# A hybrid attention and convolution block: the decay gates' matmuls are moved from between two quads to inside the next one

## The chip, the core and the metric

The kernel runs on one NeuronCore of a Trainium2 chip. The metric is the device time of one execution in microseconds; the time before is the median of three runs. The engines are TensorE (PE in the profile), VectorE (DVE), ScalarE (ACT), GpSimd (POOL) and SyncE (SP, which only issues DMAs here).

## What is computed

One layer on a sequence of 1024 tokens of width 1024, all in float32: an RMS norm, one wide input projection, then side by side a gated linear attention in both directions (4 heads, keys of 128, values of 256) and a gated convolution of width 3; both results are concatenated, projected back, added to the input and normed once more. Cut to the parts that the change touches:

```python
proj = einsum('bsd,de->bse', rmsnorm(x, norm_g), w_in)
q, k, v, z_a, lr_f, lr_b, b_gate, c_gate, h_c, z_c = split(proj, ...)
# the decay gates, for each direction
g_f = log_sigmoid(einsum('bsr,re->bse', lr_f, w_gk_f) + b_gk_f) / 16
# inside the attention: sums of g over each chunk of 64 tokens
b = cumsum(g, axis=3)
# the convolution group
u = c_gate * h_c
conv = conv_w[0] * u[t-1] + conv_w[1] * u[t] + conv_w[2] * u[t+1] + conv_b
y_c = b_gate * conv * silu(z_c)
```

## The kernel before

The work runs in three stages. Up to about 125 us the input is normed and turned into column tiles and the values of the heads are computed. From there to 606 us the rest of the projection is computed in twelve *quads*. After that come the attention and the output projection. The change lies in the second stage.

A quad (`quad`, line 544) computes four blocks of 128 output columns for all 1024 tokens. Each product is a Strassen-like scheme of seven products of quarter size (Winograd's form), and each float32 factor is split into a high and a low part, so that one product of two parts is three chains of matmuls. Of the seven first-level products of a block pair, one is done at a second level again, for both pairs of the quad together, with half as wide matmuls: that is `second` (line 505). So a quad is: `second` (its matmuls are 256 columns wide), then the first `pair` (line 402), then the second `pair`. The part `finish` of `second` runs inside the first pair, behind its first product.

`second` uses four banks of PSUM, `bx`, `by`, `bz` and `bw`, and writes `bx` and `by` twice. In order: line 525 (`bx`), 527 (`by`), 529 (`bz`), 531 (`bw`), 533 (`bx` again, added to what is there, after ACT's copy in line 526 has read it), 535 (`by` anew, after DVE's sum in line 528 has read it). Then the first pair's product of line 433 follows. A pair ends each of its last products with a DVE sum (`plus`, line 430); in the order of these sums the products are named p2, p7, p5 (used twice), p4 and p3. Ahead of its products a pair takes sums and differences of its raw weights on DVE (`comb`, line 407), and turns each operand into parts: a cast on ACT (line 152) and a difference on POOL (line 153).

The first eight quads are the convolution's: in the first pair the columns of c_gate and h_c, whose product `u` POOL makes (line 611); in the second pair the columns of z_c and b_gate, whose results go through `conv_y` (lines 614 to 641): the convolution (lines 619 to 621), a tanh on ACT (line 633) with two DVE operations behind it (lines 634 and 635), and a product on POOL (line 637). The other four quads compute q, k and z_a; behind their last sums stands a tanh with one DVE operation (lines 560 and 561).

The gates are cut into eight pieces, one for each head and direction, and one piece goes with each convolution quad. `gates` (line 568) does four matmuls of 64 rows and 512 columns into two banks of their own (line 577), for each half an ACT Abs (line 578) and a DVE operation (line 579) on the same bank, and one ACT Exp (line 580). `summed` (line 582) issues the ACT Ln (line 587, with a load of its table) and leaves five steps in the list `beside`: for each half a difference (line 597) and a scan of 512 (line 591 or 593), and then the DMA of `b` to DRAM (line 599). The next quad's first pair takes one step from the list behind each of its `plus` sums (`step`, line 396).

Nothing in this stage has an order written out by hand, but for `issue_after`, which queues an instruction behind another on the same engine. The framework's planner orders each engine's queue: it goes by the order of the program and by its own estimate of when operands and buffers are ready, and so may draw a later DVE operation forward into a hole. Tiles of one name take their buffers in the order of the program (`tmp` has nine). Each engine then runs its queue in order.

Of the kernel before, what the change touches and what calls it, by code (L numbers as in the profile page):

```python
# [37 lines left out]
def tile_hybrid_gla_shortconv(ctx, tc, x, norm_g, w_in, w_gk_f, b_gk_f, w_gk_b, b_gk_b,  # L38
# [40 lines left out]
    def weights(src):  # L79
        r = ws.tile([P, ND, P], F32, name="raw", bufs=4)  # L80
        r = r.rearrange("p c e -> p (c e)").rearrange("p (c e) -> p c e", e=src.shape[2])
        nc.sync.dma_start(r, src)
        return r
# [229 lines left out]
    def sums():  # L313
        for c in range(4):
            f01, f00, f11 = (joined(hb[d][s_], c) for d, s_ in ((0, 1), (0, 0), (1, 1)))
            minus(f01, f00, t1, c, f00)
            minus(f11, f01, t3, c, f01)
            minus(f11, f00, t2, c, f11)
            yield
# [21 lines left out]
    beside = sums()  # L341
# [32 lines left out]
    def s_tile():  # L374
        return ws.tile([P, 4, P], F32, name="s", bufs=3)
# [14 lines left out]
    def load(col):  # L390
        return weights(w_in[:, :, col:col + P])


    beside = []
# [110 lines left out]
    def second(x, y, h):  # L505

        b00, t1, t2, t3, b10, b11, t4 = h
        a00, a01, a10, a11 = x[:, 0:2], x[:, 2:4], y[:, 0:2], y[:, 2:4]
        f, g = s_tile(), s_tile()
        s2, s1, s3, s4 = f[:, 0:2], f[:, 2:4], g[:, 0:2], g[:, 2:4]  # L510
        o0 = part(x)
        V.tensor_tensor(s1, a10, a11, ALU.add)
        V.tensor_tensor(s2, s1, a00, ALU.subtract)
        o1 = part(f)
        V.tensor_tensor(s3, a00, a10, ALU.subtract)
        V.tensor_tensor(s4, a01, s2, ALU.subtract)
        o2 = part(g)
        o3 = part(a11)
        first_, last_ = (lambda o: tuple(a[:, 0:2] for a in o)), (lambda o: tuple(a[:, 2:4] for a in o))
        r = [wk.tile([P, 512], F32, name="r2", bufs=2) for _ in range(2)]  # L520
        lo, hi = slice(0, 256), slice(256, 512)
        w = tmp()
        p1, u = w[:, lo], w[:, hi]
        bx, by, bz, bw = (bank6()[:, lo] for _ in range(4))
        product(bx, first_(o0), b00, True, True)
        A.copy(p1, bx)
        product(by, first_(o1), t2, True, True)
        V.tensor_tensor(p1, by, p1, ALU.add)  # L528
        product(bz, first_(o2), t3, True, True)
        V.tensor_tensor(u, bz, p1, ALU.add)  # L530
        product(bw, last_(o1), t1, True, True)
        V.tensor_tensor(r[1][:, hi], bw, u, ALU.add)
        product(bx, last_(o0), b10, False, True)
        A.copy(r[0][:, lo], bx)
        product(by, o3, t4, True, True)
        V.tensor_tensor(r[1][:, lo], by, u, ALU.add)

        def finish():
            product(bw, last_(o2), b11, False, True)
            V.tensor_tensor(r[0][:, hi], bw, p1, ALU.add)  # L540

        return *r, finish

    def quad(cols_a, take_a, cols_b, take_b):
        xa, xb = load(cols_a[0]), load(cols_b[0])
        ra, rb, finish = second(xa[:, 4:8], xb[:, 4:8], h2)
        pair(xa, load(cols_a[1]), take_a, ra, finish, step)
        pair(xb, load(cols_b[1]), take_b, rb)

# [18 lines left out]
    def gates(h, d):  # L568

        bias = bgk[:, d, h:h + 1]  # L570
        dr = slice(d * 64, d * 64 + 64)
        b, m = u_tile()[:, 0:S], u_tile()[:, 0:S]
        for half in range(2):
            sl = slice(half * 512, half * 512 + 512)
            ps = bank()
            for i, w in enumerate((gk_hi, gk_lo)):
                T.matmul(ps, w[dr, h * DK:(h + 1) * DK], lr[half][dr], start=i == 0, stop=i == 1)
            A.activation(b[:, sl], ps, AF.Abs, bias=bias)
            V.tensor_scalar(m[:, sl], ps, bias, 0.0, ALU.add, ALU.min)
        return b, m, A.activation(b, b, AF.Exp, scale=-1.0)  # L580

    def summed(h, d, b, m, exp):

        with tc.issue_after(exp.ins):
            A.activation(b, b, AF.Ln, bias=1.0)

        def scan(b_, m_):
            if d == 0:  # L590
                V.tensor_tensor_scan(b_, smask, m_, 0.0, ALU.mult, ALU.add)
            else:
                V.tensor_tensor_scan(b_[:, ::-1], smask, m_[:, ::-1], 0.0, ALU.mult, ALU.add)

        for half in range(2):
            b_, m_ = (a[:, half * 512:half * 512 + 512] for a in (b, m))
            beside.append(lambda b_=b_, m_=m_: V.tensor_tensor(m_, m_, b_, ALU.subtract))
            beside.append(lambda b_=b_, m_=m_: scan(b_, m_))
        beside.append(lambda: nc.sync.dma_start(b_dram[h][d], b))
# [68 lines left out]
    for j in range(CW // P):  # L668
        u, *first_ = conv_u(j)
        args = *first_, *conv_y(j, u)  # L670
        quad(*args)
        summed(j // 2, j % 2, *gates(j // 2, j % 2))
    for h in range(NH):
        quad((Q0 + h * DK, K0 + h * DK), to_dram((q_dram[h], k_dram[h])),
             (Z0 + h * DV, Z0 + h * DV + P), silu2_to_dram(z_dram[h]))
# [373 lines left out]
```

## Time and profile before

| | |
|---|---|
| time, median of 3 runs | 901.11 us (897.99 to 902.21) |
| the profiled execution | 903.29 us, of which the span of the profile 901.2 us |
| PE busy | 865.7 us (96% of the span), 4452 matmuls |
| PE weight loads | 725.2 us (80%) |
| DVE busy | 713.4 us (79%) |
| ACT busy | 393.7 us (44%) |
| POOL busy | 448.2 us (50%) |
| mean granted TensorE clock | 0.986 of full speed |

A row of a timeline gives the start in us from the start of the span, the length in us, the engine, the line of the kernel, the operation, the tile that it writes and those that it reads, and shapes; in brackets stands how long the engine was idle before it, and which instruction it waited for. The lengths of matmuls overlap, since they are pipelined: the distance of two starts is what one costs.

### The profile page before, as it was taken

To read this page: it belongs to the slowest core of one execution; us is meant where nothing else is said; L and a number is where in the kernel's file an instruction comes from. 1 tells how busy PE (TensorE), PEld (TensorE's weight loads), DVE (VectorE), ACT (ScalarE), POOL (GpSimd) and SP (SyncE) were. 2 spreads that over 40 slices of the span, in tenths; PEclk is the share of its full clock that TensorE was granted. 3 is DMA by queue.
4 is the path that set the end of the run, shared out by engine and by line. 5 is a ranking of instruction groups with operands and counts; after the bars stand their busy time and mean duration, and the time that the engine had idled before them with its cause. 6 is when DMAs were issued, how large, how long until landed. Compare 5 with 4: busy or idle time off the path is not lost.

```text
span 901.2 us, 12971 instructions
## 1 busy us (share of the span) xinstructions
PE 865.7 (96%) x4452; PEld 725.2 (80%) x4452; DVE 713.4 (79%) x1283; ACT 393.7 (44%) x822; POOL 448.2 (50%) x391
## 2 busy tenths in 40 slices
PE   7999969999999999999999999999999999999996
PEld 6999958887887878787878888887878787888885
DVE  6879986888888888888888565666799989975754
ACT  5533233434445362635344342443365446542553
POOL 3368676757768576768665655520112212222231
PEclk9999969999999999999999999999999999999999
DMA  7521332222231313132233433468856344310122
GB/s 252 138 74 56 86 109 56 71 70 71 71 94 48 117 47 105 60 94 71 70 94 129 134 102 116 128 208 327 293 159 222 105 136 134 120 52 24 42 77 93
DMA packets 102163, 100.35 MB, mean 111 GB/s; under 512 B 10705, under 2 KB 82385, under 8 KB 101586
## 3 DMA queue, kind: packets, MB, share of 16 engines
q1 hardware_dynamic: 102098, 99.53, 35.0%
q8 instruction: 35, 0.57, 0.3%
q14 instruction: 30, 0.25, 0.1%
HBM read 71.20 MB, written 28.31 MB: 110 GB/s over the span
## 4 chain that ended last, share of the span: by engine, by line
PE 72%; DVE 17%; issue 4%; DMA 3%; POOL 2%; ACT 1%; SPq 0%; POOLq 0%; DVEq 0%; ACTq 0%
PE out L715 16%; PE pc L381 15%; PE pb L381 15%; PE pa L381 15%; PE po L872 3%; PE pu L917 2%; DVE tmp L304 1%; DVE tmp L635 1%; DVE tmp L430 1%; DVE f L304 1%; DMA k<-k_dram 1%; DVE s L407 1%; DMA raw<-in_w_in 1%; DVE xt L177 1%; DVE dd L820 1%
## 5 line engine op out<-in xcount | busy, mean ns | idle before, releaser
L153 POOL TENSOR_TENSOR a_lo<-s,a_hi 128x512 fp32r<-128x512 f32 x74 | 116.0, 1573 | 28.8 <-ACT a_hi L152 28.5
L153 POOL TENSOR_TENSOR a_lo<-tmp,a_hi 128x512 fp32r<-128x512 f32 x48 | 70.3, 1466 | 103.8 <-ACT a_hi L152 99.0
L153 POOL TENSOR_TENSOR a_lo<-raw,a_hi 128x512 fp32r<-128x512 f32 x84 | 111.2, 1327 | 14.8 <-ACT a_hi L152 14.8
L147 POOL TENSOR_TENSOR rs<-rs,mhalf 128x1 f32<-128x1 f32 x48 | 28.7, 598 | 142.6 <-DVE rs L146 135.2
L715 PE MATMUL out<-a_hi,y_hi 128*128 128x512 f32 x192 | 89.2, 465 | 0.5 <-ACT y_hi L152 0.5
L152 ACT CAST a_hi<-raw 128x512 fp32r<-128x512 f32 x108 | 63.8, 595 | 58.3 <-PE pc L381 17.2
L152 ACT CAST a_hi<-tmp 128x512 fp32r<-128x512 f32 x48 | 29.8, 621 | 122.8 <-DVE tmp L407 99.4
L715 PE MATMUL out<-a_hi,y_lo 128*128 128x512 f32 x192 | 77.1, 401 | 0.0
L715 PE MATMUL out<-a_lo,y_hi 128*128 128x512 f32 x192 | 77.0, 401 | 0.0
L827 POOL TENSOR_TENSOR kt<-kt,k 128x256 f32<-128x256 f32 x32 | 26.3, 821 | 97.7 <-ACT kt L824 70.8
L152 ACT CAST a_hi<-s 128x512 fp32r<-128x512 f32 x74 | 45.0, 617 | 47.4 <-PE pa L381 17.5
L381 PE MATMUL pa<-h_hi,a_hi 128*128 128x512 f32 (+1 forms) x128 | 47.7, 373 | 5.2 <-DVE tmp L528 2.8
L381 PE MATMUL pb<-h_hi,a_hi 128*128 128x512 f32 (+1 forms) x128 | 48.2, 376 | 4.5 <-DVE tmp L528 3.8
L381 PE MATMUL pc<-h_hi,a_hi 128*128 128x512 f32 (+1 forms) x128 | 48.0, 375 | 2.6 <-DVE tmp L528 2.6
L381 PE MATMUL pa<-h_hi,a_lo 128*128 128x512 f32 (+1 forms) x128 | 47.0, 367 | 0.7 <-POOL a_lo L153 0.7
L381 PE MATMUL pc<-h_lo,a_hi 128*128 128x512 f32 (+1 forms) x128 | 47.2, 369 | 0.0
L381 PE MATMUL pb<-h_hi,a_lo 128*128 128x512 f32 (+1 forms) x128 | 47.2, 369 | 0.0
L381 PE MATMUL pc<-h_hi,a_lo 128*128 128x512 f32 (+1 forms) x128 | 47.1, 368 | 0.0
L381 PE MATMUL pb<-h_lo,a_hi 128*128 128x512 f32 (+1 forms) x128 | 47.1, 368 | 0.0
L381 PE MATMUL pa<-h_lo,a_hi 128*128 128x512 f32 (+1 forms) x128 | 46.8, 365 | 0.0
L715 PEld LDWEIGHTS out<-a_hi,y_lo 128*128 128x128 f32 x192 | 36.4, 190 | 8.0
L717 DVE TENSOR_TENSOR res<-out,res 128x512 f32<-128x512 f32 x48 | 32.9, 686 | 12.4 <-PE out L715 12.3
(344 smaller groups left out, 2735.2 us busy)
## 6 DMA issues: line engine op xcount, KB each, us to landing
raw<-in_w_in SPq DMA_DIRECT2D x56, 512.0 KB, 4.0
raw<-in_w_out SPq DMA_DIRECT2D x16, 512.0 KB, 3.9
xt<-in_x SPq DMA_DIRECT2D x8, 512.0 KB, 8.4
yc_dram<-tmp SPq DMA_DIRECT2D x16, 256.0 KB, 2.0
b_dram<-u SPq DMA_DIRECT2D x8, 512.0 KB, 2.6
z_dram<-tmp SPq DMA_DIRECT2D x16, 256.0 KB, 2.4
s<-yc_dram SPq DMA_DIRECT2D x16, 256.0 KB, 3.9
raw<-in_x SPq DMA_DIRECT2D x8, 512.0 KB, 6.7
```

Source lines behind the costliest of these rows:

```text
L147: G.tensor_tensor(rs, rs, mhalf, ALU.pow)
L152: (e_hi.copy if e_hi is A else e_hi.tensor_copy)(hi, src)
L153: e_lo.tensor_tensor(lo, src, hi.bitcast(F32), ALU.subtract)
L177: V.scalar_tensor_tensor(xts[t][:, sl], xts[t][:, sl], rs, gb[:, sl], ALU.mult, ALU.mult)
L304: V.tensor_tensor(f, blk[0].bitcast(F32)[:, c], blk[1].bitcast(F32)[:, c], ALU.add)
L381: T.matmul(ps, a[x0][:, k], b_[x1][:, k], start=start and k == 0 and j == 0, stop=stop and k == n - 1 and j == 2, skip_group_check=not start)
L407: V.tensor_tensor(f, x0, x1, op)
L715: T.matmul(ps, a[:, j, :], w, start=j == 0 and i == 0, stop=j == 3 and i == 2)
L717: V.tensor_tensor(res[t][:, cs], ps, (xr if row0 == NT else res[t])[:, cs], ALU.add)
L827: G.tensor_tensor(kk, kk, k4, ALU.mult)
L872: T.matmul(o, l, m, start=j == 0, stop=j == len(mm) - 1)
L917: T.matmul(pu[:, d], ks[:, d], r["v"][:, t], start=True, stop=True)
```

## The change

In the convolution's quads the call of `gates` and `summed` moves from behind the quad into it, between `second` and the first pair. In the list `beside` an empty step goes ahead of the other steps, so that the first sum of the pair (behind p2) takes nothing, and the two differences, the two scans and the DMA stand behind the following sums, of the same quad as the gates.

```diff
-    def quad(cols_a, take_a, cols_b, take_b):
+    def quad(cols_a, take_a, cols_b, take_b, aside=lambda: None):
         xa, xb = load(cols_a[0]), load(cols_b[0])
         ra, rb, finish = second(xa[:, 4:8], xb[:, 4:8], h2)
+        aside()
         pair(xa, load(cols_a[1]), take_a, ra, finish, step)
         pair(xb, load(cols_b[1]), take_b, rb)
...
+        beside.append(lambda: None)
         for half in range(2):
             b_, m_ = (a[:, half * 512:half * 512 + 512] for a in (b, m))
             beside.append(lambda b_=b_, m_=m_: V.tensor_tensor(m_, m_, b_, ALU.subtract))
             beside.append(lambda b_=b_, m_=m_: scan(b_, m_))
         beside.append(lambda: nc.sync.dma_start(b_dram[h][d], b))
...
         u, *first_ = conv_u(j)
         args = *first_, *conv_y(j, u)
-        quad(*args)
-        summed(j // 2, j % 2, *gates(j // 2, j % 2))
+        quad(*args, lambda: summed(j // 2, j % 2, *gates(j // 2, j % 2)))
```

The amount of work on each engine stays the same. The first gates' matmuls now stand in the first quad instead of behind it, and the last in the eighth quad instead of ahead of the first Q/K quad.

## Rows read from the trace of the kernel before

**Rows 1.** PE's waits from 124 to 606 us: engine, bank and line, releaser: total, times, longest us

```profile
PE pb L381 <- DVE tmp L528: 3.8, 3, 1.9
...
PE pb L381 <- ACT tmp L526: 0.6, 1, 0.6
```

**Rows 2.** Timeline of PE near 207 us: start, length, operation, tiles, count [idle before]

```profile
204.99 0.49 PE L577 MATMUL out<-y_hi 64*128 64x512 f32 x1
...
206.11 0.39 PE L381 MATMUL pc<-h_hi,a_hi 128*128 128x256 f32 x1
...
209.65 0.28 PE L381 MATMUL pc<-h_hi,a_lo 128*128 128x256 f32 x1
210.84 0.38 PE L381 MATMUL pa<-h_hi,a_hi 128*128 128x256 f32 x1 [0.91 <-DVE tmp L528]
...
217.86 0.39 PE L381 MATMUL pc<-t_hi,a_hi 128*128 128x512 f32 x1
```

**Rows 3.** Timeline of DVE at the same place

```profile
206.68 0.68 DVE L430 TENSOR_TENSOR tmp<-pb,tmp 128x512 f32<-128x512 f32 x1
207.28 0.73 DVE L579 TENSOR_SCALAR u<-out,bgk 128x512 f32<-128x512 f32 x1
208.05 0.69 DVE L634 SCALAR_TENSOR_TENSOR th<-th,tmp 128x512 f32<-128x512 f32 x1
...
209.32 1.13 DVE L635 SCALAR_TENSOR_TENSOR tmp<-th,tmp 128x512 f32<-128x512 f32 x1
210.37 0.41 DVE L528 TENSOR_TENSOR tmp<-pa,tmp 128x256 f32<-128x256 f32 x1
```

**Rows 4.** Timeline of ACT at the same place

```profile
207.39 0.63 ACT L633 ACTIVATE th<-tmp 128x512 f32<-128x512 f32 x1 [0.95 <-DVE tmp L430]
...
208.49 0.37 ACT L526 COPY tmp<-pc 128x256 f32<-128x256 f32 x1
...
211.13 1.06 ACT L587 ACTIVATE u<-u 128x1024 f32<-128x1024 f32 x1
```

**Rows 5.** Timeline of POOL at the same place

```profile
206.88 1.31 POOL L153 TENSOR_TENSOR a_lo<-raw,a_hi 128x512 fp32r<-128x512 f32 x1
208.14 1.76 POOL L637 TENSOR_TENSOR tmp<-tmp 128x512 f32<-128x512 f32 x1
```

**Rows 6.** Timelines of DVE and POOL near 203 us

```profile
202.62 1.19 DVE L407 TENSOR_TENSOR s<-s,raw 128x512 f32<-128x512 f32 x1
203.73 1.23 DVE L407 TENSOR_TENSOR s<-raw 128x512 f32<-128x512 f32 x1
203.22 1.19 POOL L153 TENSOR_TENSOR a_lo<-raw,a_hi 128x256 fp32r<-128x256 f32 x1
```

**Rows 7.** Timeline of DVE between two Q/K quads

```profile
568.11 0.69 DVE L430 TENSOR_TENSOR tmp<-pb,tmp 128x512 f32<-128x512 f32 x1 [0.38 <-PE pb L381]
568.72 1.75 DVE L407 TENSOR_TENSOR tmp<-raw 128x512 f32<-128x512 f32 x1
570.40 0.68 DVE L561 SCALAR_TENSOR_TENSOR tmp<-tmp 128x512 f32<-128x512 f32 x1
571.00 0.41 DVE L528 TENSOR_TENSOR tmp<-pa,tmp 128x256 f32<-128x256 f32 x1
```

**Rows 8.** Timeline of DVE: the last product's sum at two other boundaries

```profile
165.00 0.67 DVE L430 TENSOR_TENSOR tmp<-pa,tmp 128x512 f32<-128x512 f32 x1
...
453.19 0.68 DVE L430 TENSOR_TENSOR tmp<-pb,tmp 128x512 f32<-128x512 f32 x1
```

**Rows 9.** Chain of work: start us, us, what; 18 matmuls of lines 535 and 433 together

```profile
170.39 3.73 PE pc L381 x18
...
292.93 5.29 PE pc L381 x18
...
457.35 3.74 PE pa L381 x18
```

**Rows 10.** PE by stretches of 2 us: stretch, PE busy (x), granted clock, DMA share, GB/s

```profile
294.00:296.00 2.00, 2.00 (x8) 0.50 0.08 30
```

## The prediction

> **What bounds the kernel now.** I read the page first (span, busy shares), then the list of who waited for whom on PE between 124 and 606 us, the chain of work, and last the timelines of PE, DVE, ACT and POOL around one place. PE is the bound: from 130 us to 606 us it runs almost without a gap. The list of its waits names one kind that counts, a product waiting for DVE's line 528, nine times, up to 1.9 us [rows 1] (one of three such lines, by the bank, with three waits each, and the only line of another kind). The first of the nine (at 128 us) is the start of the stage, before any quad's gates; the other eight stand at the eight places where a quad follows a convolution quad. I call these boundaries 1 to 8; boundary 2, near 207 us, is the model. Between two Q/K quads, where no gates stand, the list has no such wait.
>
> Boundary 2 on PE [rows 2]: the four gate matmuls run from 204.99 to 206.11 (1.12 us), then `second`'s first 30 narrow matmuls (lines 525 to 533) from 206.11. The last of them starts at 209.65, so they take 0.122 us each and PE could start line 535 at 209.77, which is 3.66 us after 206.11. It starts at 210.84. Line 535 writes the bank `by` anew, and so has to wait until line 528 has read it. PE thus loses 1.07 us here, with the gates' 1.12 us already spent ahead of it.
>
> Why line 528 is late [rows 3, 4, 5]: DVE runs the last product's sum (L430) at 206.68, then a gate operation (L579) at 207.28, L634 at 208.05 when ACT's tanh has come (207.39 + 0.63), the other L579, L635 at 209.32, and line 528 at 210.37. L635 takes 1.13 us because POOL holds the SBUF: POOL's second L637 ends at 208.14 + 1.76 = 209.90, and L635 ends 0.55 us after that. That POOL and DVE take turns is seen elsewhere [rows 6]: of two DVE operations back to back (202.62 and 203.73, 1.2 us each) the second waits for POOL's operation, which started between them and itself waited for the first. The Trainium skill (SBUF — State Buffer, section "SBUF: two separate sides") states that this pair of ports is an exclusive lock for a whole instruction. By that rule the trace agrees. The rows alone say that taking away the two L579 frees less than their length, since L635 ends with POOL and not with DVE's queue.
>
> From L430's start to line 535's start it is 210.84 - 206.68 = 4.16 us in boundary 2 and 457.35 - 453.19 = 4.16 us in boundary 8 [rows 2, 3, 8, 9]; the five between agree within 0.01. Boundary 1, where DVE isn't behind, has 170.39 - 165.00 = 5.39 us.
>
> **The change part by part.** *The gate matmuls on PE* (4 x 8) keep their number. They leave the eight boundaries ahead of `second` and go behind line 535. Ahead, their 1.12 us passed while DVE worked towards line 528: they were cover. Behind line 535 nothing is late (the rest of the quad has no wait), so each quad pays 1.12 us there: 8 x 1.12 = +8.96 us. Against it stands x, by which line 535 starts earlier after the end of the last quad. The change of the time is 8.96 minus the sum of the eight x.
>
> *What DVE does without the two L579.* PE comes to line 535 at 204.99 + 3.66 = 208.65. Line 528 is issued in the order that the planner gives DVE. The trace of before doesn't show this boundary without gates, but three Q/K boundaries are without them: there DVE has L430, L407 (a difference of raw weights for the next pair, 1.75 us beside POOL), L561 behind the tanh, L528, L407 [rows 7]. So while the tanh runs, L407 fills the hole in which L579 stood. Why not before: L407's `tmp` comes behind the one that ACT's line 526 fills (208.49, rows 4), and with 1.12 us of gate matmuls ahead that came too late. I take the same order with L634 for L561: L430, L407, L634, L528, L635. In boundary 2: L407 from 207.28, held until POOL's L153 ends (206.88 + 1.31 = 208.19), done 0.55 later at 208.74. POOL's L637, ready since 208.14, now takes its turn: 1.25 us, to about 209.95. L634 waits for that and ends 0.55 later at 210.5, line 528 runs 210.42 to 210.83, and line 535 starts at 210.88. So x = 210.84 - 210.88, about zero. The two L579 are gone and L407 and the lock have their place. This holds too if L407 isn't drawn in and L635 stays ahead of line 528: L637 follows L634, L635 follows L637, as before. Line 528 comes early only with no more than one locked operation in front of it. POOL's order around it hangs on the same L430, so boundaries 2 to 8 have x = -0.04 each. In boundary 1, POOL is further ahead relative to PE; the same steps give L407 to 167.0, L637 to 168.25, L634 to 168.8, line 535 at 169.2: x = 1.2. Sum of x: 1.2 - 7 x 0.04 = 0.9; **+8.0 us**.
>
> The bounds of x from both sides: at best line 535 doesn't wait at all, x = 210.84 - 208.65 = 2.19 in boundary 2 (19.7 over the eight, from the same rows of each); at worst three locked operations stand ahead (L407, L634, L635), each further one costing POOL's 1.25 and its own 0.55, x = -1.8.
>
> *PE's clock.* In boundary 4 two waits stood close, 0.6 us for ACT's L526 [rows 1] and the usual one for L528, and after them the granted clock was 0.50, the 1.2 GHz level, between 294 and 296 us [rows 10]; the 18 matmuls then took 5.29 us for 3.73 [rows 9], 1.56 us more. At boundaries 1 and 8, with one wait of under 1 us, the 18 took 3.73 and 3.74. In my order L533 waits for L526 (behind the tanh: 207.39 + 0.63 + 0.37, less overlap, 208.3 for 207.83: 0.45 us) and then line 535 for 1.9 us: more idle than boundary 4 had. The Trainium skill (TensorE: Matmul & The Clock Gate, section "What's actually happening") says that TensorE's idle state is the slow one and activity releases it. I take three more falls in seven boundaries, the middle between none and all: 3 x 1.56 = **+4.7 us**; range 0 to 10.9.
>
> *ACT's gate work* (two Abs, Exp, table, Ln) moves into the first pair. Before, it ends 7.2 us after the first gate matmul (212.19 - 204.99, rows 2, 4), with other work between. After, it would end at most 0.82 (line 535) + 7.2 = 8.0 us after line 535's start. The first sum (L597) stands on DVE behind p7's sum. p7's product starts 217.86 - 210.84 + 1.12 = 8.14 us after line 535 and ends 2.75 later, so the Ln is done and no DVE queue is held. If the casts for p7 stood wholly behind the Ln, PE would wait there up to 1.8 us (a pass of ACT like the tanh's 0.63, POOL's lower half 1.31: 9.94 for 8.14); I take zero, because its L407 now comes earlier and the cast is ready before the Abs. Range 0 to 1.8 a quad.
>
> *L579, sums and DMA.* Two L579 (2 x 0.73 us) and the later sums meet idle DVE in the first pair; p3's sum comes later by up to a scan, and POOL's product into `u` stands behind lower halves of the second pair's casts anyway, so the convolution isn't later. `b_dram`'s DMA moves back on SP as far as the last scan does, with the raw loads behind it, which are for the next quad: zero. Lost cover: if the convolution did get later, every us would come on L430 of the next boundary and on the end. In quad 0 the gates might fill the 1.9 us wait of the start: 0 to -1.1 us.
>
> Sum: 8.0 + 4.7 = +12.7 us. The profiled run took 903.29 us (span 901.20 and 2.09 around it), so 916.0 of the same kind; its median of three is 901.11, 2.2 lower, so **913.8 us** as median, 1.4% slower.
>
> **Rivals.**
> *Line 528 comes first (faster).* If the planner sees line 528 ready during the tanh, or puts L407 behind L634, one locked operation at most stands ahead of it. Then L634 runs at 208.05, L528 at 208.66 to 209.07, line 535 at 209.13: x = 1.7, in boundary 1 about 2.0; 8.96 - 7 x 1.7 - 2.0 = -4.9 us, and -6.5 if boundary 4's clock fall goes: 895 to 896. Without any wait 8.96 - 19.7 = -10.7: 890. It decides from line 528 standing ahead of the second locked operation. For it: the Q/K boundaries have no PE wait, and without gates `by` is done by 206.6. Against: their order on DVE, with L407 first, and POOL's L637, which they lack.
> *The gates fill the wait (no change).* The planner may issue the gate matmuls ahead of line 535, or the lock lets L634 pass straight behind L407 (line 535 at 209.75, x about 1.1). Then the 1.12 is covered again: -1 to +4 us, 900 to 905.
> *Line 528 behind all three (much slower).* 8 + 7 x 1.8 = +20.6 and clock falls: 922 to 932.
>
> **How the numbers follow.** Forecast 0.53 (its own range 905 to 921), line 528 first 0.27, no change 0.13, all three 0.07. Some 0.5% is what a measurement of this kernel tells from none, 4.5 us. Faster 0.27, same 0.13, slower 0.60. For 8 in 10 the range reaches down over most of the fast case, 895, and up to 921, leaving out the waitless case and the very slow one.
>
> **What would show it.** Right: DVE in a boundary reads L430, L407, L634, L528; PE's wait at line 535 is near 1.9 us instead of 0.9; L577 stands behind line 535; more stretches with a clock of 0.50. Wrong: waits at line 535 under 0.5 us, or L577 ahead of it; a PE wait for a cast at p7; in boundary 2, L430 later after the last product than now (206.68 - 204.99 = 1.69 us).

## The result and the profile after

| | before | predicted | after |
|---|---|---|---|
| time, median | 900.58 us in the same series | 913.8 (895 to 921) | 955.17 us (951.84 to 957.32) |
| ratio to before | | 1.014 | 1.060 (95% interval 1.0577 to 1.0624) |
| span of the profiled execution | 901.2 us | | 949.8 us |
| mean granted clock | 0.986 | | 0.959 |

The change makes the kernel 6.0% slower. The forecast had the sign and a quarter of the size (12.7 of 54.6 us), and the time lies outside its range. The profiled execution before lies above its median and the one after is the fastest of its four, so their spans differ by only 48.6 us. In the profile after, the matmul of the gates is line 578 (was 577), the operation behind the tanh 636 (634), the next one 637 (635), POOL's product 639 (637); line 535, 528, 526, 430 and 407 keep their numbers.

PE's waits in the same stage (engine, bank and line <- releaser: total us, times, longest us), to be read beside [rows 1]:

```profile
PE pc L381 <- DVE tmp L528: 13.7, 3, 4.6
PE pa L381 <- DVE tmp L528: 13.7, 3, 4.6
PE pb L381 <- DVE tmp L528: 10.4, 3, 4.6
```

It is the same wait at the same nine places. At the eight boundaries it is now 4.6 us instead of 0.7 to 1.0; the first of the nine, at the start of the stage, is 1.3 instead of 1.9. Boundary 2 on PE (start, length, what, and in brackets the idle time before), as [rows 2]:

```profile
211.17 0.28 PE L381 MATMUL pc<-h_hi,a_hi 128*128 128x256 f32 x1
...
219.74 0.58 PE L381 MATMUL pa<-h_hi,a_hi 128*128 128x256 f32 x1 [4.55 <-DVE tmp L528]
...
221.31 0.79 PE L578 MATMUL out<-y_hi 64*128 64x512 f32 x1
...
228.33 0.40 PE L381 MATMUL pb<-t_hi,a_hi 128*128 128x512 f32 x1
```

`second` begins at 211.17, line 535 waits until 219.74, the gates stand behind it at 221.31, and the first product behind `finish` starts at 228.33. DVE at the same place, as [rows 3]:

```profile
213.96 0.68 DVE L430 TENSOR_TENSOR tmp<-pb,tmp 128x512 f32<-128x512 f32 x1
214.56 1.45 DVE L407 TENSOR_TENSOR tmp<-raw 128x512 f32<-128x512 f32 x1
215.93 1.75 DVE L407 TENSOR_TENSOR tmp<-raw,s 128x512 f32<-128x512 f32 x1
217.60 1.75 DVE L636 SCALAR_TENSOR_TENSOR th<-th,tmp 128x512 f32<-128x512 f32 x1
219.27 0.41 DVE L528 TENSOR_TENSOR tmp<-pa,tmp 128x256 f32<-128x256 f32 x1
219.61 1.44 DVE L637 SCALAR_TENSOR_TENSOR tmp<-th,tmp 128x512 f32<-128x512 f32 x1
```

Between the last sum and line 528 stand three operations that need their turn against POOL, which has no gap there (as [rows 5]):

```profile
214.16 1.29 POOL L153 TENSOR_TENSOR a_lo<-raw,a_hi 128x512 fp32r<-128x512 f32 x1
215.41 1.72 POOL L639 TENSOR_TENSOR tmp<-tmp 128x512 f32<-128x512 f32 x1
217.09 1.71 POOL L153 TENSOR_TENSOR a_lo<-s,a_hi 128x512 fp32r<-128x512 f32 x1
```

The three end 0.56, 0.55 and 0.55 us behind the end of POOL's three (216.01 for 215.45, 217.68 for 217.13, 219.35 for 218.80), so each costs a whole operation of POOL. ACT, as [rows 4]:

```profile
212.05 0.37 ACT L526 COPY tmp<-pc 128x256 f32<-128x256 f32 x1 [0.25 <-PE pc L381]
214.67 0.63 ACT L635 ACTIVATE th<-tmp 128x512 f32<-128x512 f32 x1 [2.25 <-DVE tmp L430]
```

Line 526's copy now stands ahead of the tanh, at 212.05; before it stood behind the tanh, and so it does at the three Q/K boundaries. The product that it reads is now first in `second`'s row, with no gate matmuls ahead; that the planner changed the order for this reason is likely, not shown. The granted clock of PE by stretches (stretch, PE busy, PEld, DVE, ACT, POOL busy, clock, DMA share, GB/s), as [rows 10]:

```profile
211.20:219.70 8.50, 3.86 (x31) 3.46 (x29) 8.50 (x10) 2.74 (x5) 7.27 (x6) 1.00 0.17 46
219.70:228.30 8.60, 8.56 (x28) 6.60 (x29) 5.12 (x7) 6.33 (x9) 4.25 (x5) 0.61 0.47 139
228.30:258.60 30.30, 30.30 (x135) 24.90 (x134) 26.65 (x29) 10.38 (x17) 19.47 (x13) 1.00 0.19 53
```

Behind the wait PE runs at 0.61 of full speed on average, that is mostly at the 1.2 GHz level (the stretch 221 to 225 reads 0.50), until the next product; then at full speed to the next boundary. It is so at all eight boundaries (0.56 to 0.66 over the same stretch).

One boundary with its quad, from these rows and the same places of before (204.99, 210.84 and the product at 215.12):

| boundary 2 | before | forecast | after |
|---|---|---|---|
| last product's end to line 535 | 5.85 | 5.89 | 8.57 |
| line 535 to the product behind `finish` | 4.28 | 5.40, with a clock fall 6.96 | 8.59 |
| rest of the quad | 30.30 | 30.30 | 30.23 |

So nothing is lost in the rest of the quad; 2.72 us are lost ahead of line 535, 1.12 are the gates behind it, and 3.19 are the clock. Over all eight, from boundary 1 to the first Q/K boundary, the stage takes 541.91 - 164.23 = 377.7 us for 491.86 - 164.77 = 327.1 before, 50.6 us more. The same rows of each boundary add up to it: 19.3 us ahead of line 535 (1.7 to 2.9 each), 7 x 1.12 = 7.8 for the gates (behind boundary 8 stands a Q/K quad, which has none), 24.1 for the clock (25.7 less the fall that boundary 4 had before already), and 0.7 less in the rest of the quads.

### The profile page after: what moved, and what is told of

The parts are those of the page before. It is cut to its first block, busy times and chain, and to the rows that moved or that the text cites. A ratio compares the mean times of both kernels' runs of the same rounds, so it can differ in the third digit from the quotient of the medians.

```text
span 949.8 us, 12963 instructions
## 1 busy us (share of the span) xinstructions
PE 885.3 (93%) x4452; PEld 740.2 (78%) x4452; DVE 752.5 (79%) x1283; ACT 397.4 (42%) x822; POOL 460.5 (48%) x391
## 4 chain that ended last, share of the span: by engine, by line
PE 63%; DVE 24%; issue 4%; DMA 4%; POOL 2%; ACT 2%; SPq 0%; POOLq 0%; DVEq 0%; ACTq 0%
PE out L716 14%; PE pa L381 13%; PE pc L381 13%; PE pb L381 13%; PE po L873 3%; DVE tmp L407 3%; DVE th L636 3%; DVE tmp L430 2%; PE pu L918 2%; PE out L578 2%; DMA b<-b_dram 2%; DVE tmp L622 1%; DVE tmp L623 1%; DVE tmp L304 1%; DVE f L304 1%
## 5 line engine op out<-in xcount | busy, mean ns | idle before, releaser
L153 POOL TENSOR_TENSOR a_lo<-tmp,a_hi 128x512 fp32r<-128x512 f32 x48 | 75.2, 1566 | 135.8 <-ACT a_hi L152 126.7
L153 POOL TENSOR_TENSOR a_lo<-s,a_hi 128x512 fp32r<-128x512 f32 x74 | 111.8, 1515 | 34.0 <-ACT a_hi L152 34.0
L153 POOL TENSOR_TENSOR a_lo<-raw,a_hi 128x512 fp32r<-128x512 f32 x84 | 119.8, 1430 | 13.9 <-ACT a_hi L152 13.9
L381 PE MATMUL pa<-h_hi,a_hi 128*128 128x512 f32 (+1 forms) x128 | 50.9, 398 | 15.9 <-DVE tmp L528 13.7
L381 PE MATMUL pc<-h_hi,a_hi 128*128 128x512 f32 (+1 forms) x128 | 50.4, 394 | 13.7 <-DVE tmp L528 13.7
L381 PE MATMUL pa<-h_hi,a_lo 128*128 128x512 f32 (+1 forms) x128 | 49.5, 386 | 0.9 <-POOL a_lo L153 0.9
L381 PE MATMUL pa<-h_lo,a_hi 128*128 128x512 f32 (+1 forms) x128 | 49.3, 385 | 0.0
L381 PEld LDWEIGHTS pa<-h_hi,a_hi 128*128 128x128 f32 x128 | 26.4, 206 | 22.4 <-DVE tmp L528 14.3
L430 DVE TENSOR_TENSOR tmp<-pc,tmp 128x512 f32<-128x512 f32 x48 | 32.3, 682 | 14.0 <-PE pc L381 13.9
```

The costliest lines, as they stand in the source:

```text
L153: e_lo.tensor_tensor(lo, src, hi.bitcast(F32), ALU.subtract)
L381: T.matmul(ps, a[x0][:, k], b_[x1][:, k], start=start and k == 0 and j == 0, stop=stop and k == n - 1 and j == 2, skip_group_check=not start)
L430: step(V.tensor_tensor(f, ps, x, ALU.add))
```

## The experiments

I call *lag* the time from the end of the last product on PE (start of the matmul behind it) to the start of its sum on DVE. It is 206.68 - 204.99 = 1.69 us at boundary 2 before [rows 2, 3], 1.7 to 2.6 at boundaries 2 to 8, and 0.23 at boundary 1; in the changed kernel it is 2.7 to 2.8 at all eight. Lags of other runs are told for boundaries 2 to 8.

### The change in two halves

*The empty step alone* (sums one place later, gates where they were):

```diff
+        beside.append(lambda: None)
         for half in range(2):
```

> The gates stay behind the quad as in the kernel before; only the empty step is added, so the differences and scans stand one sum later in the next quad's first pair. Queue theory (line 528 waits on DVE behind operations drawn ahead of it): DVE's order at the boundary stays that of before, so 898 to 904 us. Rival (the later sums put DVE behind in the second pair, and that lag comes out at the boundary): the lag of 1.1 us that the changed kernel shows would be here too, 8 x 1.1 = 9 us more, 909 or above.

Measured: 908.01 us, ratio 1.0077 (1.0051 to 1.0103), so +7 us where the prediction had put zero. DVE's order at the boundary is that of before, so the first theory's 898 to 904 missed, and the time comes just under its rival's 909: the lag is 2.6 to 3.4 us. The lags add 5.9 us over the seven boundaries, and a second fall of the clock, at boundary 6, 1.6. PE now waits for line 526 as well, whose copy stands behind the tanh that waits for the late sum:

```profile
PE pc L381 <- ACT tmp L526: 2.9, 3, 1.4
```

In the quad itself one thing has changed ahead of that, on DVE: the second pair's second L407 (`raw,s`), which stood behind the last scan and one sum at 228.01 - 204.99 = 23.0 us after the end of the last product before, now has the second scan between it and the first, and starts 227.17 - 202.40 = 24.8 us after it.

```profile
224.84 0.69 DVE L407 TENSOR_TENSOR tmp<-raw 128x512 f32<-128x512 f32 x1
...
226.04 1.22 DVE L593 TENSOR_TENSOR_SCAN u<-smask,u 128x512 f32<-128x512 f32 x1
227.17 1.73 DVE L407 TENSOR_TENSOR tmp<-raw,s 128x512 f32<-128x512 f32 x1
```

*The gates moved alone* (the call as in the change, no empty step):

> The gates move into the quad as in the changed kernel, but without the empty step: the sums stand behind p2, p7, p5, p5. Queue theory: the two differences L407 still go ahead of the tanh's operation and of line 528, so 948 to 960 us, waits of about 4.5 us at line 535. Rival (later sums): back towards 945 or less by the 9 us above.

Measured: 946.65 us, 1.05 (1.0469 to 1.0532): +45.7, just under the range expected. DVE draws the same two L407 ahead of line 528, and line 535 again starts 5.8 us after the last sum. But the lag is 1.8 us at all eight boundaries, where the changed kernel has 2.7 to 2.8, and the waits are 3.9 us for 4.6: the last microsecond of lag in the changed kernel comes with the sums' later place, not with the move. The two halves add up to 52.8 of the 54.6 us. The move makes the bulk, and the sums' place is a small price of its own.

### Where the 46 us of the move go

*The two L407 queued behind line 528*, in the changed kernel:

```diff
+        with tc.issue_after(read_by[0].ins):
-        os3 = part(comb(t4_(), a00, a10, ALU.subtract))
+            os3 = part(comb(t4_(), a00, a10, ALU.subtract))
... (the same for os4; read_by[0] is line 528)
```

> The changed kernel, but the first pair's third and fourth differences (L407) are queued behind line 528 on DVE. Queue theory: line 528 now follows the last sum directly, PE hardly waits at line 535 and keeps its clock; eight boundaries at (204.99 + 3.66 for 210.84) 2.2 to 2.5 us less and 1.12 us more for the gates than before: 888 to 897 us, faster than before. Rival (ACT's gate work or the sums in the first pair hold PE): the time stays above 930, with PE waiting elsewhere.

Measured: 907.29 us, 1.006 (1.0037 to 1.0083). No product waits for line 528 any more, so the order of DVE behind the last sum carries 48 of the 54.6 us, most of the clock's share among them. The gates behind line 535 stay uncovered (5.6 us from it to the product behind `finish` at boundary 2, where before had 4.28). It does not reach the 888 to 897 that I expected: the lag grew to 3 to 5.4 us, and PE waits at the next banks of `second` instead (line 432 is the sum, 430 elsewhere):

```profile
PE pc L381 <- DVE tmp L432: 5.7, 4, 2.2
PE pb L381 <- DVE tmp L432: 4.6, 5, 1.5
PE pa L381 <- DVE tmp L432: 3.3, 3, 1.4
```

*POOL's product at the boundary on 1 of 512 columns*, in the changed kernel (`y[:, 0:1]` in line 639); the outputs lack the rest of it:

> The changed kernel, but POOL's product of the convolution (line 639) works on 1 column of 512; the rest of that product is left out. Lock theory: of the three DVE operations between the last sum and line 528 the first two no longer wait for POOL; line 528 stands 2 to 3 us nearer to that sum than the 5.3 us of the changed kernel, and 8 x 2.5 us or more go: 925 to 937. Rival (the three are that slow by themselves, or wait for tanh): the distance stays above 4.5 us, above 945.

Measured: 929.45 us, 1.0311 (1.0268 to 1.0353), as the theory of turns has it. POOL has two such products at a boundary, one for each half. Line 528 comes 3.45 us behind the last sum instead of 5.3, though no operation on DVE was changed:

```profile
211.97 0.68 DVE L430 TENSOR_TENSOR tmp<-pb,tmp 128x512 f32<-128x512 f32 x1
212.57 1.73 DVE L407 TENSOR_TENSOR tmp<-raw 128x512 f32<-128x512 f32 x1
214.23 0.68 DVE L407 TENSOR_TENSOR tmp<-raw,s 128x512 f32<-128x512 f32 x1
214.83 0.68 DVE L636 SCALAR_TENSOR_TENSOR th<-th,tmp 128x512 f32<-128x512 f32 x1
215.43 0.41 DVE L528 TENSOR_TENSOR tmp<-pa,tmp 128x256 f32<-128x256 f32 x1
```

The second L407 and L636, 1.75 us each in the changed kernel, take 0.68 here, where POOL's product is over in 0.2 us. This run also shows what a wait costs behind itself. PE waits 2.7 us at each of the eight boundaries, and behind line 535 the clock stays up at three of them and falls at the five others; boundaries 1 and 2, from line 535 on:

```profile
173.40:179.00 5.60, 5.58 (x28) 4.49 (x29) 5.01 (x7) 4.58 (x7) 4.27 (x5) 1.00 0.55 148
215.90:224.60 8.70, 8.70 (x29) 6.62 (x29) 4.97 (x7) 6.46 (x9) 4.30 (x6) 0.61 0.55 151
```

The same matmuls take 5.59 us at the one and 8.70 at the other. So a wait of one length can cost 3.1 us of slow clock or none.

*The gates inside the wait*, between lines 533 and 535 of the changed kernel:

```diff
+        aside()
         product(by, o3, t4, True, True)
... (the call behind `second` goes)
```

> The changed kernel with the gates' matmuls one product earlier, between line 533 and line 535, in the wait itself; DVE's order stays. Queue theory: line 535 starts when it did, the 1.12 us of gates is hidden, 8 x 1.12 = 9 us less, 943 to 947; if the four matmuls are enough to keep the clock up, up to 8 x 3.2 us less again, 920. Rival (gate work in the first pair): it starts earlier by the wait's length, so most of the loss goes, below 915.

Measured: 930.17 us, 1.0312 (1.0281 to 1.0342), between the two figures of the first theory. The wait is 3.5 us at most boundaries instead of 4.6, and the mean clock 0.978 instead of 0.959: 25 us come back, of which 8 x 1.12 = 9 are the cover and the others mostly clock: the 8.6 us behind line 535 read 0.82 for 0.61,

```profile
215.40:224.00 8.60, 8.60 (x37) 7.40 (x38) 5.71 (x9) 5.63 (x8) 6.70 (x7) 0.82 0.49 140
```

*The wait filled with matmuls*: thirty narrow matmuls into a bank that nobody reads, at the same place, at the eight boundaries:

```diff
+        if filled[0]:
+            ps = bank()[:, lo]
+            for _ in range(5):
+                product(ps, first_(o0), b00, True, True)
         product(by, o3, t4, True, True)
... (`filled` is off for the first quad and on from the second to the first Q/K quad)
```

> The changed kernel, with 30 narrow matmuls (3.7 us at full clock) added in each of the eight waits, between line 533 and line 535, into a bank that nobody reads. If the slow matmuls after the wait come from the clock, line 535 starts as before and the clock stays near 1.0 behind it: 8 x 3.2 us less, 926 to 934. Rival (line 535 to the first pair is slow for another reason, or the wait follows PE's work): 955 or more.

Measured: 932.9 us, 1.0349 (1.0307 to 1.0391). PE does more work and the kernel is 22 us faster than the changed one. Line 528 still comes 8.1 us after the last product, so DVE gained nothing. PE's idle time ahead of line 535 is down to 1.1 us, and the stretches around boundary 2 (the second one begins with line 535, at 219.8) read 1.00 where the changed kernel has 0.61:

```profile
219.88 0.39 PE L381 MATMUL pa<-h_hi,a_hi 128*128 128x256 f32 x1 [1.09 <-DVE tmp L528]
...
211.30:219.80 8.50, 7.43 (x61) 7.02 (x59) 8.50 (x11) 3.04 (x6) 6.81 (x5) 1.00 0.16 43
219.80:228.30 8.50, 8.42 (x41) 6.81 (x42) 5.78 (x10) 6.90 (x10) 5.75 (x7) 1.00 0.49 143
```

So the idle of 4.6 us costs, beside itself, 22 / 8 = 2.8 us of slow clock at each boundary on average, near the 3.19 of the table.

### Why a shorter wait at the boundary gains nothing

*The two L407 behind line 528 and the sums at their old place* (the edit of the second part above without the empty step):

> As e3_combs_behind (gates moved, the two L407 of the first pair behind line 528), but the sums stand where they stood, behind p2 to p5, without the empty step. e1_sums_later cost 7 us by itself. If what e3 keeps over the kernel before (6.3 us) is that, 898 to 902 us here. Rival (it is the L407, which now come late and hold up the first pair's casts, so POOL's product into u and the convolution): 904 to 908 as e3, with line 430's last sum still 4 us or more behind the last product.

Measured: 907.31 us, 1.0073 (1.0047 to 1.01). The time is in the rival's 904 to 908, with lags up to 5.6 us.

*The kernel before with the gated operation L635 of the second pair queued behind line 528*:

```diff
-        V.tensor_tensor(p1, by, p1, ALU.add)
+        read_by = V.tensor_tensor(p1, by, p1, ALU.add)
+        while late:
+            with tc.issue_after(read_by.ins):
+                late.pop(0)()
... (`conv_y` leaves the second half's L635 in the list `late`)
```

> The kernel before, with one thing changed: the last DVE operation of the convolution's gating (line 635, the one ahead of line 528) is queued behind line 528. Lock theory: line 528 then follows the second line 579 and not POOL's end plus 0.55 us; line 535's wait of 1.0 us goes at seven or eight boundaries, and the clock fall of boundary 4 with it: 890 to 895 us. Rival (the wait comes from something behind it, as the bank of bz or ACT's copy): 899 to 902.

Measured: 901.73 us, 1.0006 (0.999 to 1.0021). Line 528 did come 1.1 us closer to the last sum, and PE now waits for line 526 (up to 1.7 us) with a lag of 3.3 to 3.7: quads of 41.0 us on average, as before. Twice a wait was removed and the last sum came later by as much. So the convolution quads seem to be held at some 41 us by something behind PE, and the boundary only shows it.

First theory: POOL's product for the second half of `u` (line 611), sixth in a row of POOL's, and the convolution behind it.

```diff
-                G.tensor_tensor(u[:, 1 + o:513 + o], kept[0, half], kept[1, half], ALU.mult)
+                (V if half else G).tensor_tensor(u[:, 1 + o:513 + o], kept[0, half], kept[1, half], ALU.mult)
```

This edit was made in four kernels: before,

> The kernel before with one operation moved from POOL to DVE: the product that makes the second half of u (512 columns) in a convolution quad. In the kernel before it stands on POOL in order behind three lower-half differences and runs about 3 us after its input, and ACT's cast of it, DVE's convolution and the second pair's sums follow it. Theory (a loop DVE, POOL, ACT, DVE holds the quads at some 41 us): the convolution ends some 3 us earlier against the last product, the last sum stands within 0.2 to 1 us of the last product at every boundary (before 1.7 to 2.6), the wait for line 528 is 0.5 to 0.9 us and boundary 4 keeps its clock: 893 to 897 us. Rival (DVE is simply full and each further operation on it adds to its lag): the last sum no earlier, 901 to 906 us.

before with L635 queued behind line 528,

> As the run before, and the second pair's last L635 is queued on DVE behind line 528. Without the loop's relief that second edit brought nothing (901.73 for 900.58 us), as the last sum came later by what the wait lost. Loop theory: with the lag gone line 528 comes under 2.5 us after the last sum and no product waits at the boundary for more than 0.4 us, quads of about 39.2 to 39.8 us: 886 to 893 us, and under both kernels. Rival (the lag has another cause): quads stay near 41 us, 899 us or more.

the changed kernel,

> The changed kernel with the same product of u on DVE. DVE's order at the boundary is unchanged (last sum, two L407, the gated operation, line 528), so the wait behind the last sum (5.3 to 5.8 us from it to line 535), the clock fall behind it and the uncovered gate matmuls should stay; what can go is the lag of the last sum behind the last product (2.75 us in the changed kernel to 0.5 to 1). Loop theory: 935 to 945 us, with waits of 2.5 to 3 us at line 535. If the lag alone had made the change slow: under 915. If the lag has nothing to do with the product of u: 953 to 958.

and the one with the two L407 behind line 528 and the sums at their old place.

> Gate matmuls inside the quad as in the changed kernel, their sums at the old place, the first pair's two late L407 queued on DVE behind line 528, and the product of u on DVE. Without the last of these it ran 907.31 us, with the last sum up to 5.6 us behind the last product and waits of about 2 us in place of the one removed. Loop theory: lag and those waits go, and the place of the gates costs nothing any more: 888 to 896 us. Rival (the late L407 delay the casts of the first pair by themselves, whatever makes u): 903 to 908 us.

Measured: 902.6, 901.17, 955.75 and 910.1 us (ratios 1.0027, 1.0008, 1.061, 1.0102). All four miss the theory's range; the first three lie in their rivals', the last 2 us above its rival's. The lag is 1.9 to 2.8 us in the first, 2.4 to 3.6 in the second, 3.1 to 3.2 in the third and 4.4 to 5.9 in the fourth. In the first, DVE's busy time in a quad goes up from 34.9 to 37.8 us (mean of the six quads from boundary 2 to 8), for a product that takes 1.08 us in the quad behind boundary 2: the other operations take longer. The theory falls.

Second theory: DVE with its turns simply has too much to do. *The kernel before without the third tap of the convolution* (line 621 taken out), and *the kernel with the two L407 behind line 528 without it*:

> The kernel before without L621, the third tap of the convolution (two DVE operations a quad, 0.74 to 2.1 us with their turns); the outputs lack that tap. DVE's order at the boundary is the same. Theory (DVE, with the turns it waits for POOL, is as full as PE in a convolution quad: between the second product of the first pair and line 528 it has about 33 us of work in 33 us): with some 2.1 us less the last sum comes within 0.2 to 0.5 us of the last product at all eight boundaries (before 1.7 to 2.6 at boundaries 2 to 8), boundary 4 keeps its clock, quads of 39.3 to 40.2 us: 890 to 896 us. Rival (the lag comes from a chain over POOL and ACT and not from DVE's own work): the last sum stays 1.5 us or more behind, 899 to 902 us.

> The changed kernel with the two late L407 behind line 528 (907.29 us, last sum up to 5.4 us behind the last product, waits of about 2 us in the banks behind), now also without the third tap, which the outputs lack. DVE-full theory: those waits were the same lack of room on DVE, so they shrink by the 2.1 us and the last sum comes within 3.3 us: 888 to 895 us, within 4 us of the kernel before without its third tap. Rival (late casts for the first pair make the waits, whatever DVE has to do): 900 to 907 us.

Measured: 898.1 us (0.9977, 0.9952 to 1.0002) and 902.53 us (1.002). Two operations less brought 2.5 us, no more than the noise, and 4.8 us; the second lies in its rival's range. In the first boundary 4 keeps its clock, as expected, but the lag stayed at 1.8 to 2.4 us. DVE's busy time fell by only 0.6 us a quad, from 34.9 to 34.3, and not by the 2.1 expected. *The gate as one Silu on ACT and one product on DVE*, with nothing left out:

```diff
-                A.activation(th, ap, AF.Tanh, scale=0.5)
-                V.scalar_tensor_tensor(th, th, 1.0, ap, ALU.add, ALU.mult)
-                V.scalar_tensor_tensor(y, th, 0.5, y, ALU.mult, ALU.mult)
+                A.activation(th, ap, AF.Silu)
+                V.tensor_tensor(y, th, y, ALU.mult)
```

> The kernel before with the gate of the convolution written as one Silu on ACT and one product on DVE, in place of a tanh on ACT and two operations on DVE (L634 and L635). Nothing is left out. It takes 2 x 0.69 us off DVE in each convolution quad, half of it between the last sum and line 528. DVE-full theory: line 528 comes 0.6 us or more earlier behind the last sum and the sum itself earlier by up to 0.7: waits at the boundary under 0.3 us, quads near 39.5 us, 888 to 896 us, under both kernels. Rival (something else keeps quads at 41 us, as in the four runs that took work away at the boundary alone): 898 to 903 us; a dearer table on ACT would show as a wait of line 526's copy.

Measured: 904.63 us, 1.0042 (1.0027 to 1.0057); lag 2.3 to 3.2, though DVE is busy 32.5 us a quad, 2.3 less. ACT loads three tables a quad instead of two (1.28 us each), and PE now waits for line 526's copy at some boundaries (up to 1.2 us), the sign that the expectation named. *The third tap scaled by ACT and added by POOL*:

> The kernel before with the convolution's third tap made by ACT (a scaled copy into another buffer) and added by POOL in place of one DVE operation each. Nothing is left out. DVE has two operations a quad less, POOL two more that take the same turns, and the second stands behind POOL's differences of the second pair. DVE-full theory with POOL's turns as part of what fills it: less than the run without the tap gives, 894 to 900 us. If DVE's own time alone counted: as the run without the tap. If POOL becomes the late one: 902 us or more, with the last convolution sum waiting for POOL.

Measured: 915.5 us, 1.0165, in the range of the third alternative, with a lag of 3.1 to 4.1 us. None of these runs brought the last sum forward by taking work off DVE in the second pair. None is a clean test either: the tap freed little, the Silu added tables, and the last run added to POOL.

Third theory: what stands ahead of the second pair's first L407 in DVE's queue. In the kernel before, in the quad behind boundary 2, DVE and then POOL:

```profile
225.70 1.21 DVE L593 TENSOR_TENSOR_SCAN u<-smask,u 128x512 f32<-128x512 f32 x1
226.83 0.67 DVE L407 TENSOR_TENSOR tmp<-raw 128x512 f32<-128x512 f32 x1
```

```profile
228.30 1.55 POOL L153 TENSOR_TENSOR a_lo<-tmp,a_hi 128x512 fp32r<-128x512 f32 x1 [6.78 <-ACT a_hi L152]
...
235.67 1.74 POOL L611 TENSOR_TENSOR u<-tmp 128x512 f32<-128x512 f32 x1
```

The first L407 of the second pair stands behind both scans of the gates. POOL has nothing to do for 6.78 us until that L407 and its cast are done, and then works off a row of operations, the product of `u` among them, against which DVE has to take turns up to the boundary. *The kernel before without the sums* (one column of each difference is left, no scans):

> The kernel before without the gates' differences on full width and without the scans (one column of each difference stays); the gates' decays are left out of the outputs. DVE has some 4 us less in each quad, and the first L407 of the second pair no longer stands behind the scans. Theory (the sums' place ahead of that L407 is what makes POOL, the convolution and the last sum late): the last sum stands within 0.5 us of the last product at all boundaries, quads of 39.2 to 40.2 us: 888 to 895 us. Rival (the turns of POOL and DVE in the second pair hold the lag whatever comes ahead of them): last sum 1.5 us or more behind, 898 to 901 us.

Measured: 892.64 us, 0.9906 (0.9879 to 0.9933), as the theory expected. POOL, the convolution and the last sum are early:

```profile
225.12 1.49 POOL L153 TENSOR_TENSOR a_lo<-tmp,a_hi 128x512 fp32r<-128x512 f32 x1 [5.66 <-PE pb L381]
...
232.24 1.29 POOL L611 TENSOR_TENSOR u<-tmp 128x512 f32<-128x512 f32 x1
```

```profile
223.62 0.68 DVE L407 TENSOR_TENSOR tmp<-raw 128x512 f32<-128x512 f32 x1
...
244.32 0.69 DVE L430 TENSOR_TENSOR tmp<-pc,tmp 128x512 f32<-128x512 f32 x1 [0.20 <-PE pc L381]
```

The last sum waits for its product (the bracket), with a lag of 244.32 - 244.22 = 0.10 us, the same at all boundaries but the first (0.22); quads take 39.8 to 40.0 us for 40.4 to 42.9 (behind boundaries 2 to 8). Two operations less, later in DVE's queue, left the lag where it was; the sums less, ahead of L407, take it away. They also take more off DVE than any run above: it is busy 29.9 us a quad, 5.0 less. *The sums behind the second pair's products* (the second `pair` gets `step` instead of the first), nothing left out:

> The kernel before with the gates' sums (two L597 and two scans, some 4.3 us of DVE) put behind sums of the quad's second pair instead of the first. Nothing is left out. In every convolution quad so far POOL is without work for 6.8 to 8.2 us, up to some 23 to 25 us after the last product of the quad before (30 in the changed kernel), until DVE's first L407 of the second pair, which stands behind the second scan, and then has seven operations back to back, the product of u sixth. Theory (DVE's order makes POOL late, and POOL's backlog makes the convolution and the last sum late): L407 comes 2 us earlier, the gap closes by 2 us, and the last sum comes within 1 us of the last product unless the sums now in its way take it back: 892 to 899 us. Rival (sums in the second pair stand ahead of the last sums and cost their own length there): last sum 4 us behind, 903 to 912 us.

Measured: 935.64 us, 1.0379 (1.036 to 1.0398), worse than its rival's 903 to 912. The sums now stand in the last sums' way (a scan between them, in DVE's rows below), the lag is 4.7 us, and both kinds of wait are long:

```profile
250.06 0.68 DVE L430 TENSOR_TENSOR tmp<-pa,tmp 128x512 f32<-128x512 f32 x1
250.66 1.70 DVE L593 TENSOR_TENSOR_SCAN u<-smask,u 128x512 f32<-128x512 f32 x1
252.28 0.66 DVE L430 TENSOR_TENSOR tmp<-pb,tmp 128x512 f32<-128x512 f32 x1
...
PE pc L381 <- ACT tmp L526: 8.1, 3, 2.7
...
PE pa L381 <- DVE tmp L528: 3.6, 3, 1.4
```

So the 4 us of sums have to go somewhere on DVE, and the place in the kernel before is the best of the three that were run. Taking them away moves both their place and their length, so which of the two counts within the first pair stays open, and with it whether DVE is late by its order or by its load. No version that computes everything was faster than the kernel before.

## Why the prediction was right in direction and wrong in size

The step that failed is x, the time by which line 535 starts earlier: forecast at +0.9 us over the eight boundaries, measured at -19.3 (-2.72 at boundary 2). It has two parts, DVE's order behind the last sum and the lag ahead of it. The clock, whose price was taken for three boundaries, was missed by about as much again. Part by part:

- *What bounds the kernel* held: PE waits at line 535 for line 528 and nowhere else in the stage, and nothing in the rest of the quad changed (30.30 and 30.23 us).
- *The gates behind line 535 are uncovered*: right; they stand at 221.31 behind 219.74, and where the clock stays up (the filled wait) they take 1.13 us there.
- *x is about zero because L407 and the turns take the place of L579*: the mechanism was right, the count was not. I took the order over from the Q/K boundaries, where one L407 stands ahead of line 528 [rows 7]; DVE took two, ahead of the operation behind the tanh. I had line 526's copy behind the tanh (208.3 us), as it is there. In the changed kernel it stands ahead of the tanh (212.05 for 214.67); since the `tmp` of the late L407 come behind the one that it fills, this may be what opens the hole for both, but it was not tried by itself. With three operations to take turns, the last sum to line 535 is 5.78 us (213.96 to 219.74) instead of 4.16 [rows 2, 3]. The rival with three operations had the right count (with L635 as the third) and 1.8 us for one more, which the 1.62 bear out, but it was given a chance of 0.07, and with the lag held constant and the clock underpriced its 922 to 932 us came out too low as well. That this order carries the bulk is shown by the run with the two L407 behind line 528 (48 us less).
- *The lag* was held constant: 1.69 became 2.79 us, the other 1.1 us of the 2.72. The run with the move alone has 1.8, so this part comes from the sums' later place. The prediction named a later L430 as a sign that it would be wrong, and so it was.
- *The clock*: the fall was expected at three boundaries for 1.56 us each, 4.7 us in all, at most 10.9. It came at all eight, for 2.8 to 3.8 us at boundaries 1 to 7 and 2.0 at boundary 8, 25.7 us in all, and the run with the filled wait got 22 back. The price was taken from boundary 4, where the waits were 0.6 and 0.95 us [rows 1, 9, 10]; behind 4.6 us the slow stretch cost twice as much at most boundaries. It is not the length alone that sets it: with waits of 2.7 us (POOL's short product) the same matmuls took 3.1 us more at boundary 2 than at boundary 1, where the clock stayed up.
- *Sums and their DMA cost nothing*: wrong by 7 us, by the run with the empty step alone. I looked at p3's sum and at the product of `u`, and not at what the sums push back in DVE's queue: the second pair's second L407. That this L407 alone makes the 7 us is argued, and 1.6 of them are a further fall of the clock; the run without the sums shows that place and length of the sums in the first pair cost some 8 us together.
- *ACT's gate work costs nothing*: right, PE waits for no cast at p7.

The turns are told by the Trainium skill too (SBUF — State Buffer, section "SBUF: two separate sides"): the shared port of GpSimd and VectorE is locked for a whole instruction. By that the three ends 0.55 us behind POOL's agree, and so does the run with POOL's short product (0.68 us for 1.75).

## What to carry to other kernels

Work that an engine does while another is awaited is cover: before moving it, ask what the planner will draw into the hole, and count all that fits, not one. Price a longer wait together with the clock behind it: here 3.6 us of idle more (4.55 for 0.91) brought 3.2 us of slow matmuls at boundary 2. And where removing a wait at one place lengthens the lag at another by as much, look for what the late engine does earlier: here taking out the sums ahead of the next pair's first operand on DVE removed the lag, while the edits at the place of the wait brought no kernel below the one before.

## What was not expected of the hardware

- Idle TensorE time can be paid a second time. Behind a wait of 4.6 us the granted clock was 0.61 on average for 8.6 us; with thirty useless matmuls in that wait, and 1.1 us of idle left, it stayed at 1.00 and the kernel was 22 us faster. Behind waits of 2.7 us the same matmuls ran at 1.00 at one boundary and at 0.61 at the next.
- An operation of 0.68 us on DVE took 1.75 beside a POOL without gaps. Shortening POOL's two products at a boundary took 1.85 us off DVE's path there (5.3 to 3.45 us) and 26 us off the changed kernel; giving DVE one of POOL's operations gained nothing.
- A gate by one Silu on ACT with one product on DVE was no faster than a tanh with two: 904.63 for 900.58 us, with one table load of 1.28 us more in each quad.
